# The two norms of a transformer block taken apart: raw x is transposed, g scales the transposed operand, rstd scales the products

## The chip, the cores and the metric

The kernel runs on one core of a Trainium2 chip. Its time is device time in microseconds (us). TensorE (PE) multiplies, VectorE (DVE) and ScalarE (ACT) do elementwise work, GpSimd (POOL) takes a small share of it, and SyncE (SP) issues the DMA transfers.

## What is computed

Two transformer blocks run one after the other over 256 tokens of width 1024, each with two layers, all in float32. The change touches the second block, whose layer is:

```python
def _rmsnorm(x, g):
    return x * lax.rsqrt(jnp.mean(x * x, axis=-1, keepdims=True) + NORM_EPS) * g

def _layer(x, ...):
    h = _rmsnorm(x, g_mix)
    proj = h @ w_in          # queries, keys, values of three attentions, gates
    ...
    x = x + y @ w_out
    h2 = _rmsnorm(x, g_mlp)
    x = x + jnp.square(jax.nn.relu(h2 @ w_up)) @ w_down
    return x
```

After the second layer a last rmsnorm with g_final gives the output. In what follows rstd is the factor rsqrt(mean(x²)+eps), one number for each token, and g is one number for each of the 1024 channels.

## The kernel before

**Tiles.** The 256 tokens are two tiles of 128 (tb 0 and 1), and each 1024 wide row is two halves of 512 (c 0 and 1). A float32 product is three matmuls on operands split into a high and a low part (mm3, L290 to L292). A split is an ACT copy that rounds to the high part (L297) and a DVE subtraction that leaves the low part (L298). Since TensorE contracts over partitions, the normed x has to be transposed before it is an operand: transposed4 (L441) puts four 128x128 transposes into a PSUM bank ("sm" in the rows), and the split reads that bank.

**Weights.** They stream in units of 512 KB (128 x 1024), loaded six units ahead of use and split three ahead: ACT copies (L265), DVE subtracts (L267). A table SLOW gives the subtraction of four units at each place between two stages to POOL instead of DVE. The ACT copy of such a unit is what releases the POOL subtraction.

**The norm.** norm_g(x, hT, tb, g) does everything for one token tile: sum_sq squares both halves on ACT (L430), rms_scale adds the two sums (L435) and runs six more operations on 128x1 tiles for rsqrt on DVE (L409, L413, L418, L413, L420, L421); then for each half DVE writes x * rstd * g (L570), PE transposes it (L441), and ACT and DVE split it (L297, L298). It is called at four places, which I call B1 to B4:

- B1, from the first block into the second (ev_out, L1216 to L1226). Here the residual add (L1224) itself needs an rms_scale of the first block's own norm first.
- B2, from attention to MLP in layer 0 (ev_out, residual add L1725).
- B3, from the MLP of layer 0 to the attention of layer 1 (end, residual add L1776).
- B4, from attention to MLP in layer 1 (as B2).

**Order.** In proj(), token tile 1 runs a few weight units behind tile 0 (lag), so that tile 0's first matmuls of the next stage can cover tile 1's norm. A scheduler decides the order of the instructions of each engine when the program is built, from the written order and its own estimates; on the chip each engine runs its queue strictly in that order.

Of the kernel before, what the change touches and what calls it, by code (L numbers as in the profile page):

```python
# [100 lines left out]
def two_block_kernel(ctx: ExitStack, tc: tile.TileContext, A, out):  # L101
# [299 lines left out]

    def rsqrt(v, n, c):
# [18 lines left out]
        dve.scalar_tensor_tensor(y, t, 5.0 * r ** 4, y, op0=ALU.add, op1=ALU.mult)  # L421
        return y

# [7 lines left out]

    def rms_scale(sq, n=1):
# [3 lines left out]
        return rsqrt(v, n, D ** 0.5)  # L436

# [125 lines left out]

    def norm_g(x, hT, tb, g):
        sq = small(2)
        sum_sq(x, sq)
        rs = rms_scale(sq, 1)
        for c in range(2):
            xn = t2([P, 512])
            dve.scalar_tensor_tensor(xn, x[c], rs, g[c], op0=ALU.mult, op1=ALU.mult)  # L570
            yield from transpose_half(hT, tb, c, xn)

# [249 lines left out]
    def block1_layer(l, hT, xin, t_norm):  # L822
# [387 lines left out]
        def ev_out(c, tb, ps):  # L1210
# [9 lines left out]
            if last:  # L1220
                x = new[tb]
                rs = rms_scale(sqs[i][:, 0:2], 1)
                for c in range(2):
                    dve.scalar_tensor_tensor(x[c], osb.pop((tb, c)), rs, x[c], op0=ALU.mult, op1=ALU.add)  # L1224
                run(norm_g(x, nxt, tb, g_mix0))
            elif i == 1:  # L1226
                tbs = (2 * s, 2 * s + 1)
                g = update_affine([new[t] for t in tbs], [[osb.pop((t, c)) for c in range(2)] for t in tbs],
                                  sqs[s], nxt, s, mods)
                if s == 0:  # L1230
                    run(g)
                else:
                    later.append(spawn(g))

        if last:
            g_mix0 = load_g(A["g_mix_2"][0])
        proj(4, ya, ev_out, groups=2, lag={1: LAGB} if last else {2: LAG0, 3: LAG0})
        return nxt, new, later

# [63 lines left out]

    def merge_tok(bi, acts, waits, oT, operands, y, yT):


        for c in range(2):
            gt = {}

            def ev_gate(tb, ps):  # L1310
                t = gt[tb] = t2([P, 512])
                act.activation(t, ps, AF.Tanh, scale=0.5)
            if c == 0:
# [83 lines left out]

    def block2_layer(l, hT):
        acts = {tb: hT.stat(tb) for tb in range(2)}

        brT = {}
# [47 lines left out]
        def qc_task(tb, z):  # L1449
# [6 lines left out]
            for i in range(2):  # L1456
                split(*(t[:, :, tb * P:(tb + 1) * P] for t in qcT[i]), pt[:, 2 * i:2 * i + 2])

        def ev_qc(tb, ps):
            z = t2([P, 512])  # L1460
            act.activation(z, ps, AF.Copy, scale=0.125)
            t_c.append(spawn(qc_task(tb, z)))
# [9 lines left out]
        tailT = t2([P, 256])  # L1472
        act.activation(tailT, ps, AF.Copy)
        tail = {}
# [107 lines left out]
        def ev_qb(q, ps):  # L1582
            split(*qbT[q], ps, scale=0.125)
        projT(4, hT.mov, ev_qb)

        def ev_kb(q, ps):
            for j in range(2):
                r = slice(64 * j, 64 * j + 64)
# [29 lines left out]

        def ev_qa(q, ps):
            for j in range(2):  # L1620
                r = slice(64 * j, 64 * j + 64)
                split(*(t[r, :, j] for t in qbdA[q]), ps[r], scale=0.125)
        projT(4, hT.mov, ev_qa)
        kaT = [(t2([P, 2, 256], F32R), t2([P, 2, 256], F32R)) for _ in range(2)]

        def ev_ka(q, ps):
            split(*kaT[q], ps)
        projT(4, hT.mov, ev_ka)
        va = {}
# [124 lines left out]
        def down(f, uT, lag):  # L1754
            w = {}
            for step in range(4 + lag):
# [4 lines left out]
                for tb in range(2):  # L1761
# [7 lines left out]
                    for k in range(2):  # L1769
# [107 lines left out]
```

## Time and profile before

| | |
|---|---|
| Time, median of 3 runs | 1871.62 us (1869.54 to 1873.0) |
| Profiled execution | 1872.96 us, of which span 1871.1 us |
| Mean granted TensorE clock | 0.990 of full speed |
| Busy time of PE / DVE / ACT / POOL | 1817.4 / 1217.6 / 872.9 / 200.9 us |
| Share of the 16 DMA engines | 44.5% |

The span runs from the first to the last recorded instruction. Busy time is summed over an engine's instructions. PE is busy in 97% of the span, so what can be gained is what PE waits for, plus what it loses at a lower clock. All rows below are from the one profiled execution.

### The profile page before, as it was taken

The numbers are of one execution on the slowest core, as the hardware profiler recorded it, in microseconds if no ns is written. First come the engines' busy times: TensorE is split into PE (matmuls) and PEld (weight loads), VectorE is DVE, ScalarE is ACT, GpSimd is POOL, SyncE is SP. The second block draws the span as 40 slices with busy tenths as digits, with TensorE's granted clock in tenths as the row PEclk, the third lists the DMA queues.
The fourth block names the chain that finished last, engine by engine and source line by source line (L and its number), as shares of the span: only waits on it lengthen the run. The fifth ranks groups of instructions, "written<-read, shape, count | busy, mean of one in ns | idle before, by whom it ended". The sixth has DMA issues, their size and how long they took to land.

```text
span 1871.1 us, 25763 instructions
## 1 busy us (share of the span) xinstructions
PE 1817.4 (97%) x9696; PEld 1520.0 (81%) x9696; DVE 1217.6 (65%) x2356; ACT 872.9 (47%) x1507; POOL 200.9 (11%) x135
## 2 busy tenths in 40 slices
PE   8999999999999999999989999999998999989998
PEld 4888888887887878878878887789987878779997
DVE  4754546567876744578779886555567988655555
ACT  4623233445334433465455675434455567534443
POOL 2020000001101110001020033100012003220000
PEclk9999999999999999999999999999999999999999
DMA  9433224323463332446733355545553345554552
GB/s 354 142 124 120 94 70 131 104 91 113 147 214 102 120 102 78 146 139 213 257 124 136 126 180 170 178 147 187 185 187 134 122 141 171 180 168 147 191 182 100
DMA packets 80604, 281.42 MB, mean 150 GB/s; under 512 B 9824, under 2 KB 10208, under 8 KB 80352
## 3 DMA queue, kind: packets, MB, share of 16 engines
q1 hardware_dynamic: 80480, 279.78, 44.5%
q8 instruction: 76, 1.25, 0.3%
q14 instruction: 48, 0.39, 0.1%
HBM read 278.69 MB, written 1.05 MB: 150 GB/s over the span
## 4 chain that ended last, share of the span: by engine, by line
PE 74%; DVE 9%; ACT 2%; issue 1%; POOL 1%; DVEq 0%; ACTq 0%; POOLq 0%
PE mm L290 19%; PE mm L291 18%; PE mm L292 18%; PE sm L290 3%; PE sm L291 3%; PE sm L292 3%; DVE k L267 2%; PE sm L441 1%; PE sm L1155 1%; PE sm L1128 1%; POOL k L1684 1%; PE sm L1393 1%; DVE nw_t L413 1%; PE sm L1382 1%; DVE k L1556 1%
## 5 line engine op out<-in xcount | busy, mean ns | idle before, releaser
L290 PE MATMUL mm<-k,k 128*128 128x512 f32 (+1 forms) x2192 | 837.2, 382 | 2.2 <-ACT k L465 2.2
L291 PE MATMUL mm<-k,k 128*128 128x512 f32 (+1 forms) x2192 | 824.6, 376 | 0.9 <-POOL k L267 0.9
L292 PE MATMUL mm<-k,k 128*128 128x512 f32 (+1 forms) x2192 | 824.1, 376 | 1.1 <-DVE k L267 0.8
L267 DVE TENSOR_TENSOR k<-k,k 128x1024 fp32r<-128x1024 f32 x437 | 541.5, 1257 | 184.4 <-ACT k L265 120.0
L265 ACT ACTIVATE k<-k 128x1024 fp32r<-128x1024 f32 x458 | 474.3, 1056 | 346.0 <-DVE k L267 138.1
L290 PEld LDWEIGHTS mm<-k,k 128*128 128x128 f32 x2192 | 415.3, 190 | 77.5 <-issue 5.8
L292 PEld LDWEIGHTS mm<-k,k 128*128 128x128 f32 x2192 | 414.6, 189 | 76.5 <-DVE k L467 1.3
L291 PEld LDWEIGHTS mm<-k,k 128*128 128x128 f32 x2192 | 415.5, 190 | 70.2 <-POOL k L267 1.8
L290 PE MATMUL sm<-k,k 128*128 128x256 f32 (+1 forms) x504 | 148.5, 295 | 0.0
L291 PE MATMUL sm<-k,k 128*128 128x256 f32 (+1 forms) x504 | 146.5, 291 | 0.0
L292 PE MATMUL sm<-k,k 128*128 128x256 f32 (+1 forms) x504 | 145.8, 289 | 0.0
L267 POOL TENSOR_TENSOR k<-k,k 128x1024 fp32r<-128x1024 f32 x21 | 51.5, 2472 | 463.4 <-ACT k L265 351.2
L290 PEld LDWEIGHTS sm<-k,k 128*128 128x128 f32 x504 | 96.7, 192 | 3.6 <-issue 2.4
L1749 DVE TENSOR_TENSOR k<-k 128x512 f32<-128x512 f32 x28 | 19.3, 688 | 121.7 <-ACT k L1748 121.7
L291 PEld LDWEIGHTS sm<-k,k 128*128 128x128 f32 x504 | 96.6, 192 | 2.0 <-issue 0.3
L292 PEld LDWEIGHTS sm<-k,k 128*128 128x128 f32 x504 | 96.6, 192 | 1.0
L619 DVE CUSTOM_DVE_ANT_0 k<-k,k 128x1024 f32<-128x1024 f32 x56 | 68.9, 1234 | 22.6 <-PE mm L291 20.2
L1748 ACT ACTIVATE k<-sm 128x512 f32<-128x512 f32 x28 | 16.5, 590 | 131.5 <-PE sm L292 131.5
L297 ACT ACTIVATE k<-sm 128x256 fp32r<-128x256 f32 (+2 forms) x102 | 41.2, 410 | 77.1 <-PE sm L441 50.9
L298 DVE TENSOR_TENSOR k<-sm,k 128x256 fp32r<-128x256 f32 (+2 forms) x102 | 45.7, 458 | 37.1 <-ACT k L297 30.3
L441 PE MATMUL sm<-cst,k 128*128 128x128 f32 x232 | 38.3, 293 | 23.5 <-DVE k L570 20.0
L441 PEld LDWEIGHTS sm<-cst,k 128*128 128x128 f32 x232 | 29.1, 150 | 35.2 <-issue 25.9
(284 smaller groups left out, 1577.9 us busy)
## 6 DMA issues: line engine op xcount, KB each, us to landing
k<-in_w_in SPq DMA_DIRECT2D x248, 512.0 KB, 3.5
k<-in_w_up SPq DMA_DIRECT2D x64, 512.0 KB, 4.4
k<-in_w_down SPq DMA_DIRECT2D x64, 512.0 KB, 3.5
k<-in_w_bo SPq DMA_DIRECT2D x48, 512.0 KB, 3.5
k<-in_w_modT SPq DMA_DIRECT2D x32, 512.0 KB, 3.5
k<-in_w_out SPq DMA_DIRECT2D x32, 512.0 KB, 3.6
k<-in_w_mod SPq DMA_DIRECT2D x16, 512.0 KB, 9.6
k<-in_c_rows SPq DMA_DIRECT2D x5, 512.0 KB, 3.7
```

The costliest lines, as they stand in the source:

```text
L265: act.activation(h, r, AF.Copy)
L267: (pool if i in slow else eng).tensor_tensor(lo, r, h.bitcast(F32), op=ALU.subtract)
L290: pe.matmul(ps, lh, rh, start=start, stop=False)
L291: pe.matmul(ps, lh, rl, start=False, stop=False)
L292: pe.matmul(ps, ll, rh, start=False, stop=stop)
L297: act.activation(h, src, AF.Copy)
L298: dve.tensor_tensor(lo, src, h.bitcast(F32), op=ALU.subtract)
L413: dve.scalar_tensor_tensor(t, y, y, v, op0=ALU.mult, op1=ALU.mult)
L441: pe.transpose(ps[:, k], src[:, k * P:(k + 1) * P], ident)
L619: dve.tensor_tensor_reduce(o, w, sb[s], 0.5, 0.0, op0=ALU.mult, op1=ALU.add, accum_out=res[:, s, i - 1:i])
L1128: pe.matmul(ps[m], a[r, h], b[r], start=(i == 0), stop=(i == 2))
L1749: dve.tensor_tensor(r, r, r, op=ALU.mult)
```

## The change

The norm is no longer applied to x before the transposes.

- scaled_half transposes the raw half of x right after its residual add. g then scales the transposed form, where a channel lies on a partition, as a scale operand of the split. As g differs for each group of 128 channels, the one ACT copy and the one DVE subtraction of 128x512 become four of each of 128x128, in pairs.
- rstd of a token is applied later, to the products. Where a product has tokens on partitions, the ACT copy out of PSUM takes rstd as its scale. Where it has tokens along the free axis (qb, kb, qa, ka, tail, and seven of eight up-projections), rstd has to lie along the free axis too: spread() transposes the broadcast rstd with two PE transposes and an ACT copy, and a DVE operation multiplies the PSUM by that row. For qb, kb, qa and ka this is an added operation (scaled()); in the up-projections the pair relu on ACT and square on DVE becomes relu with scale on DVE and square on ACT.
- The g vectors of block 2 are loaded as one tile g2 in channel-on-partition form by four small DMAs (in place of eight 256 KB broadcasts).

```diff
+    class Rms:
+        def set(self, x, tb):
+            sq = small(2)
+            sum_sq(x, sq)
+            rms_scale(sq, 1, self(tb))
+            dve.tensor_scalar(self(tb, True), self(tb), 0.5, None, op0=ALU.mult)
+        def spread(self, lead):
+            def task():
+                yield from wait(lead)
+                ps = sm_bank()[:, :256]
+                for tb in range(2):
+                    pe.transpose(ps[:, tb * P:(tb + 1) * P], self(tb).to_broadcast([P, P]), ident)
+                yield
+                self.b = t2([P, 256])
+                act.activation(self.b, ps, AF.Copy)
+            self.task = spawn(task())
...
+    def scaled_half(hT, tb, c, x, g):
+        ps = transposed4(x)
+        hh, hl = hT.dst(tb, c)
+        for k in range(4):
+            gk = g[:, 4 * c + k:4 * c + k + 1]
+            act.activation(hh[:, k], ps[:, k], AF.Copy, scale=gk)
+            dve.scalar_tensor_tensor(hl[:, k], ps[:, k], gk, hh[:, k].bitcast(F32), op0=ALU.mult, op1=ALU.subtract)
...
                     dve.scalar_tensor_tensor(x[c], osb.pop((tb, c)), rs, x[c], op0=ALU.mult, op1=ALU.add)
-                run(norm_g(x, nxt, tb, g_mix0))
+                    scaled_half(nxt, tb, c, x[c], g2[:, 0])
+                rms.set(x, tb)
...
+    g2 = cp.tile([P, 2 * DEPTH, KT], F32, name="g2")
+    for l in range(DEPTH):
+        for i, w in enumerate(("g_mix_2", "g_mlp_2")):
+            sp.dma_start(g2[:, 2 * l + i], A[w][l].rearrange("(k p) -> p k", p=P))
...
+        def scaled(ps, scale=1.0):
+            o = t2([P, 2, 256])
+            dve.scalar_tensor_tensor(o, ps, scale, rms.row()[:, None, :].to_broadcast([P, 2, 256]),
+                                     op0=ALU.mult, op1=ALU.mult)
+            return o
...
-            split(*qbT[q], ps, scale=0.125)
+            split(*qbT[q], scaled(ps, 0.125))
...
-            act.activation(vb[tb], ps, AF.Copy)
+            act.activation(vb[tb], ps, AF.Copy, scale=rms(tb))
...
+        def residual(tb, c, ps, hT, g, r):
             xs = xb[tb][c]
             dve.tensor_tensor(xs, ps, xs, op=ALU.add)
+            scaled_half(hT, tb, c, xs, g)
             if c == 1:
-                run(norm_g(xb[tb], h2, tb, g))
+                r.set(xb[tb], tb)
...
                     r = t2([P, 2, 256])
-                    act.activation(r, ps, AF.Relu)
-                    dve.tensor_tensor(r, r, r, op=ALU.mult)
+                    dve.scalar_tensor_tensor(r, ps, 0.0, rms_h.row()[:, None, :].to_broadcast([P, 2, 256]),
+                                             op0=ALU.max, op1=ALU.mult)
+                    act.activation(r, r, AF.Square)
```

**What moves in the instruction order.** The lines of the changed kernel differ: L603 and L604 are the ACT and the DVE half of a pair in scaled_half, L431 is sum_sq, L436, L409, L413, L418, L420 and L422 are rms_scale with its rsqrt, L579 is 0.5 * rstd, L442 is transposed4, L1775 is the residual add at B2 to B4. In the names, k_933 to k_936 are x (tile 0 c 0, tile 0 c 1, tile 1 c 0, tile 1 c 1).

ACT at B3, before: first all of tile 0's norm and split, then the copies (L265) of three of the four POOL units, among tile 1's squares.

```order
L430 ACTIVATE k_2472_12435,small_12434<-k_933_4669 128x512
L430 ACTIVATE k_2473_12437,small_12434<-k_934_4670 128x512
L297 ACTIVATE k_2479_12456<-sm_12451 128x4x128
L297 ACTIVATE k_2483_12467<-sm_12462 128x4x128
L265 ACTIVATE k_2486_12473<-k_2462_12396 128x1024
L430 ACTIVATE k_2495_12516,small_12515<-k_935_4673 128x512
L430 ACTIVATE k_2496_12518,small_12515<-k_936_4674 128x512
L265 ACTIVATE k_2489_12485<-k_2465_12408 128x1024
```

ACT at the same place in the changed kernel; the four L265 here are those of the four POOL units.

```order
L431 ACTIVATE k_2479_12523,small_12522<-k_933_4669 128x512
L603 ACTIVATE k_2470_12484<-sm_12479,g_5095 128x128
L265 ACTIVATE k_2473_12496<-k_2460_12442 128x1024
L603 ACTIVATE k_2470_12484<-sm_12479,g_5095 128x128
L431 ACTIVATE k_2480_12525,small_12522<-k_934_4670 128x512
L603 ACTIVATE k_2470_12484<-sm_12479,g_5095 128x128
L603 ACTIVATE k_2476_12512<-sm_12507,g_5095 128x128
L265 ACTIVATE k_2485_12540<-k_2463_12454 128x1024
L603 ACTIVATE k_2470_12484<-sm_12479,g_5095 128x128
L603 ACTIVATE k_2476_12512<-sm_12507,g_5095 128x128
L265 ACTIVATE k_2488_12552<-k_2466_12466 128x1024
```

The copies of POOL units now stand among tile 0's pairs, ahead of tile 1's squares; the first of the four, which before stood ahead of all of this, stands here too.

DVE at B3, before: tile 0's rsqrt chain, its two L570, its two splits, and the adds of tile 1 between them.

```order
L418 SCALAR_TENSOR_TENSOR nw_y_12441<-nw_t_12442,nw_y_12441 128x1
L413 SCALAR_TENSOR_TENSOR nw_t_12442<-nw_y_12441,small_12439 128x1
L420 SCALAR_TENSOR_TENSOR nw_t_12442<-nw_t_12442 128x1
L421 SCALAR_TENSOR_TENSOR nw_y_12441<-nw_t_12442,nw_y_12441 128x1
L570 SCALAR_TENSOR_TENSOR k_2477_12449<-k_933_4669,nw_y_12441,k_2230_10854 128x512
L570 SCALAR_TENSOR_TENSOR k_2481_12460<-k_934_4670,nw_y_12441,k_2231_10855 128x512
L298 TENSOR_TENSOR k_2480_12457<-sm_12451,k_2479_12456 128x4x128
L1776 TENSOR_TENSOR k_935_4673<-mm_11085,k_935_4673 128x512
L298 TENSOR_TENSOR k_2484_12468<-sm_12462,k_2483_12467 128x4x128
L1776 TENSOR_TENSOR k_936_4674<-mm_11105,k_936_4674 128x512
```

DVE at the same place in the changed kernel.

```order
L436 SCALAR_TENSOR_TENSOR small_12527<-small_12522 128x1
L409 TENSOR_SCALAR nw_y_12529<-small_12527 128x1
L604 SCALAR_TENSOR_TENSOR k_2471_12485<-sm_12479,g_5095,k_2470_12484 128x128
L604 SCALAR_TENSOR_TENSOR k_2477_12513<-sm_12507,g_5095,k_2476_12512 128x128
L413 SCALAR_TENSOR_TENSOR nw_t_12530<-nw_y_12529,small_12527 128x1
L418 SCALAR_TENSOR_TENSOR nw_y_12529<-nw_t_12530,nw_y_12529 128x1
L413 SCALAR_TENSOR_TENSOR nw_t_12530<-nw_y_12529,small_12527 128x1
L420 SCALAR_TENSOR_TENSOR nw_t_12530<-nw_t_12530 128x1
L422 SCALAR_TENSOR_TENSOR rms_10910<-nw_t_12530,nw_y_12529 128x1
L579 TENSOR_SCALAR rms_10910<-rms_10910 128x1
L604 SCALAR_TENSOR_TENSOR k_2471_12485<-sm_12479,g_5095,k_2470_12484 128x128
L604 SCALAR_TENSOR_TENSOR k_2477_12513<-sm_12507,g_5095,k_2476_12512 128x128
```

Right behind the last of these rows stands the add of tile 1, c 0 (L1775, k_935). No operation of the rsqrt chain leads to an operand of the matmuls any more, but the whole chain of tile 0 still stands ahead of tile 1's adds in DVE's queue, now among the pairs. At B2 and B4 the order is alike, with the c 0 add of tile 1 between the first L413 and L418.

PE at B3, before: tile 1's transposes (the bank's name is the one that tile 1's splits read) stand behind 18 matmuls of the next stage.

```order
L292 MATMUL mm_12556<-k_2486_12473,k_2484_12468 128x512
L290 MATMUL mm_12556<-k_2486_12473,k_2483_12467 128x512
L291 MATMUL mm_12556<-k_2487_12474,k_2483_12467 128x512
L292 MATMUL mm_12556<-k_2486_12473,k_2484_12468 128x512
L441 MATMUL sm_12532<-cst,k_2500_12530 128x128 x4
L290 MATMUL mm_12556<-k_2489_12485,k_2483_12467 128x512
L441 MATMUL sm_12541<-cst,k_2502_12539 128x128 x4
```

PE at the same place in the changed kernel.

```order
L290 MATMUL mm_11163<-k_2464_12456,k_2430_12236 128x512
L442 MATMUL sm_12575<-cst,k_935_4673 128x128 x4
L291 MATMUL mm_11163<-k_2465_12457,k_2430_12236 128x512
L292 MATMUL mm_11163<-k_2464_12456,k_2431_12237 128x512
L290 MATMUL mm_12632<-k_2467_12468,k_2470_12484 128x512
L291 MATMUL mm_12632<-k_2468_12469,k_2470_12484 128x512
L292 MATMUL mm_12632<-k_2467_12468,k_2471_12485 128x512
L290 MATMUL mm_12632<-k_2467_12468,k_2470_12484 128x512
L291 MATMUL mm_12632<-k_2468_12469,k_2470_12484 128x512
L442 MATMUL sm_12595<-cst,k_936_4674 128x128 x4
```

Tile 1's transposes moved ahead: c 0's two matmuls before the end of the down-projection (mm_11163), c 1's five matmuls into the next stage (mm_12632). Less work of PE lies ahead of them.

## Rows read from the trace of the kernel before

**Rows 1.** Waits of PE, 918 to 1871 us: total, times, longest.

```profile
PE sm L441 <- DVE k L570: 20.0, 6, 6.1
PE sm L1382 <- DVE k L1377: 2.3, 2, 1.2
```

**Rows 2.** Windows: us; busy (instructions) of PE, PEld, DVE, ACT, POOL; PEclk; DMA.

```profile
918.00:956.00 38.00, 30.51 (x133) 24.08 (x131) 27.11 (x54) 15.91 (x29) 12.13 (x7) 0.91 0.27 85
956.00:1196.00 240.00, 236.69 (x1313) 196.20 (x1312) 189.61 (x425) 141.80 (x255) 41.51 (x31) 1.00 0.48 159
1196.00:1225.00 29.00, 24.79 (x110) 20.07 (x109) 16.02 (x27) 9.94 (x17) 7.06 (x3) 0.94 0.37 127
...
1388.00:1416.00 28.00, 22.86 (x96) 18.43 (x95) 16.76 (x32) 9.64 (x18) 12.41 (x7) 0.88 0.30 97
...
1660.00:1690.00 30.00, 25.78 (x112) 20.91 (x111) 16.60 (x28) 10.27 (x19) 7.06 (x3) 0.89 0.39 123
```

**Rows 3.** Timeline at B3, DVE: start, us, instruction, idle before.

```profile
1392.74 0.69 DVE L1776 TENSOR_TENSOR k<-mm,k 128x512 f32<-128x512 f32 x1 [4.33 <-PE mm L292]
...
1399.91 0.68 DVE L1776 TENSOR_TENSOR k<-mm,k 128x512 f32<-128x512 f32 x1
...
1403.61 2.35 DVE L413 SCALAR_TENSOR_TENSOR nw_t<-nw_y,small 128x1 f32<-128x1 f32 x1
1406.00 2.26 DVE L418 SCALAR_TENSOR_TENSOR nw_y<-nw_t,nw_y 128x1 f32<-128x1 f32 x1
...
1408.94 1.41 DVE L570 SCALAR_TENSOR_TENSOR k<-k,nw_y,k 128x512 f32<-128x512 f32 x2
```

**Rows 4.** Timeline at B3, POOL.

```profile
1400.96 2.41 POOL L267 TENSOR_TENSOR k<-k,k 128x1024 fp32r<-128x1024 f32 x1 [10.30 <-ACT k L265]
```

**Rows 5.** Timeline at B3, PE.

```profile
1409.84 1.09 PE L441 MATMUL sm<-cst,k 128*128 128x128 f32 x4 [4.88 <-DVE k L570]
```

**Rows 6.** Timeline at B2, all engines.

```profile
1212.01 7.06 POOL L267 TENSOR_TENSOR k<-k,k 128x1024 fp32r<-128x1024 f32 x3 [20.93 <-ACT k L265]
...
1212.70 0.69 DVE L1725 TENSOR_TENSOR k<-mm,k 128x512 f32<-128x512 f32 x1 [0.96 <-PE mm L292]
...
1214.66 2.13 DVE L413 SCALAR_TENSOR_TENSOR nw_t<-nw_y,small 128x1 f32<-128x1 f32 x1
...
1220.67 0.63 PE L441 MATMUL sm<-cst,k 128*128 128x128 f32 x4 [4.15 <-DVE k L570]
```

**Rows 7.** Timeline at B1, DVE.

```profile
938.89 2.12 DVE L413 SCALAR_TENSOR_TENSOR nw_t<-nw_y,small 128x1 f32<-128x1 f32 x1
...
944.01 1.42 DVE L1224 SCALAR_TENSOR_TENSOR k<-k,nw_y,k 128x512 f32<-128x512 f32 x2
...
947.70 1.42 DVE L570 SCALAR_TENSOR_TENSOR k<-k,nw_y,k 128x512 f32<-128x512 f32 x2
```

**Rows 8.** Timeline at B1, PE.

```profile
948.59 1.94 PE L441 MATMUL sm<-cst,k 128*128 128x128 f32 x8 [6.12 <-DVE k L570]
950.37 0.80 PE L290 MATMUL mm<-k,k 128*128 128x512 f32 x1
```

**Rows 9.** Groups by form, DVE: count, busy us, mean ns, idle before.

```profile
L1170 DVE SCALAR_TENSOR_TENSOR k<-k,nw_y,k 128x128 f32<-128x128 f32 x24 | 7.9, 389 | 0.0
```

**Rows 10.** Groups by form, ACT.

```profile
L265 ACT ACTIVATE k<-k 128x1024 fp32r<-128x1024 f32 x458 | 474.3, 1056 | 346.0 <-DVE k L267 138.1 <-PE mm L291 83.1 <-DVE mres L619 42.7
...
L1013 ACT ACTIVATE k<-cst,lg 128x128 f32<-128x128 f32 x32 | 9.8, 390 | 0.0
```

**Rows 11.** The transposes L441, 918 to 1871 us: min/median/max ns.

```profile
L441 PE MATMUL sm<-cst,k x112: 270/273/447, 933.3 to 1696.9; 128*128 128x128 f32 x112
```

**Rows 12.** Windows of the start, columns as in Rows 2.

```profile
11.00:12.00 1.00, 0.98 (x4) 0.14 (x4) 0.06 (x1) 0.00 (x0) 0.00 (x0) 1.00 0.99 388
12.00:13.00 1.00, 0.79 (x6) 0.14 (x4) 0.00 (x0) 0.00 (x0) 0.00 (x0) 1.00 1.07 237
...
50.00:60.00 10.00, 10.00 (x49) 8.32 (x48) 6.58 (x19) 6.54 (x10) 0.00 (x0) 1.00 0.05 18
```

More of the change, by code (lines that the diff above doesn't have):

```diff
@@ L400, in projT, with rsqrt @@
                     tick()
-    def rsqrt(v, n, c):
+    def rsqrt(v, n, c, out=None):
         m, k = RSQRT[c]
@@ L420, in rsqrt @@
         dve.scalar_tensor_tensor(t, t, 10.0 / 3.0 * r ** 2, t, op0=ALU.subtract, op1=ALU.mult)
-        dve.scalar_tensor_tensor(y, t, 5.0 * r ** 4, y, op0=ALU.add, op1=ALU.mult)
-        return y
+        o = y if out is None else out
+        dve.scalar_tensor_tensor(o, t, 5.0 * r ** 4, y, op0=ALU.add, op1=ALU.mult)
+        return o
     def small(n, tag="small"):
@@ L430, in sum_sq, with rms_scale @@
             act.activation(t2([P, 512]), x[c], AF.Square, accum_out=sq[:, c * n + i:c * n + i + 1])
-    def rms_scale(sq, n=1):
+    def rms_scale(sq, n=1, out=None):
         v = small(n)
         dve.scalar_tensor_tensor(v, sq[:, 0:n], D * EPS, sq[:, n:2 * n], op0=ALU.add, op1=ALU.add)
-        return rsqrt(v, n, D ** 0.5)
+        return rsqrt(v, n, D ** 0.5, out)
     def transposed4(src):
@@ L562, in update_affine, with __init__, __call__, row @@
                 yield
[L564 to L571, printed above, removed]
+    class Rms:
+        def __init__(self):
+            self.r = T(tp, [P, 2, 2], "rms", bufs=2)
+        def __call__(self, tb, half=False):
+            return self.r[:, tb, int(half):int(half) + 1]
+        def set(self, x, tb):
[13 more added lines that the diff above has]
+            self.task = spawn(task())
+        def row(self):
+            join([self.task])
+            return self.b
+    def scaled_half(hT, tb, c, x, g):
[5 more added lines that the diff above has]
+            dve.scalar_tensor_tensor(hl[:, k], ps[:, k], gk, hh[:, k].bitcast(F32), op0=ALU.mult, op1=ALU.subtract)
     sel = C("sel")
@@ L1235, in block1_layer @@
         if last:
-            g_mix0 = load_g(A["g_mix_2"][0])
+            rms = Rms()
         proj(4, ya, ev_out, groups=2, lag={1: LAGB} if last else {2: LAG0, 3: LAG0})
-        return nxt, new, later
+        return nxt, new, rms if last else later
     class Ys:
@@ L1302, in merge, with merge_tok @@
             projT(2, operands, ev_o, n=n, ticks=1)
-    def merge_tok(bi, acts, waits, oT, operands, y, yT):
+    def merge_tok(bi, acts, waits, oT, operands, y, yT, rms=None):
         for c in range(2):
@@ L1456, in qc_task @@
             for i in range(2):
-                split(*(t[:, :, tb * P:(tb + 1) * P] for t in qcT[i]), pt[:, 2 * i:2 * i + 2])
+                split(*(t[:, :, tb * P:(tb + 1) * P] for t in qcT[i]), pt[:, 2 * i:2 * i + 2], scale=0.125)
         def ev_qc(tb, ps):
             z = t2([P, 512])
-            act.activation(z, ps, AF.Copy, scale=0.125)
+            act.activation(z, ps, AF.Copy, scale=rms(tb))
             t_c.append(spawn(qc_task(tb, z)))
@@ L1472, in block2_layer @@
         tailT = t2([P, 256])
-        act.activation(tailT, ps, AF.Copy)
+        dve.tensor_tensor(tailT, ps, rms.row(), op=ALU.mult)
         tail = {}
@@ L1582, in ev_qb @@
         def ev_qb(q, ps):
-            split(*qbT[q], ps, scale=0.125)
+            split(*qbT[q], scaled(ps, 0.125))
         projT(4, hT.mov, ev_qb)
         def ev_kb(q, ps):
+            ps = scaled(ps)
             for j in range(2):
@@ L1619, in ev_qa @@
         def ev_qa(q, ps):
+            ps = scaled(ps, 0.125)
             for j in range(2):
                 r = slice(64 * j, 64 * j + 64)
-                split(*(t[r, :, j] for t in qbdA[q]), ps[r], scale=0.125)
+                split(*(t[r, :, j] for t in qbdA[q]), ps[r])
         projT(4, hT.mov, ev_qa)
@@ L1626, in ev_ka @@
         def ev_ka(q, ps):
-            split(*kaT[q], ps)
+            split(*kaT[q], scaled(ps))
         projT(4, hT.mov, ev_ka)
@@ L1717, in block2_layer, with ev_out @@
         for bi, b in enumerate(MERGE2):
-            merge_tok(bi, acts, waits[b], [], lambda tb, b=b: by_block(brT[b])(tb), y, yT)
+            merge_tok(bi, acts, waits[b], [], lambda tb, b=b: by_block(brT[b])(tb), y, yT, rms)
         ya = {tb: yT.stat(tb) for tb in range(2)}
-        g = load_g(A["g_mlp_2"][l])
-        h2 = Acts(True)
-        def ev_out(c, tb, ps):
+        h2, rms_h = Acts(True), Rms()
+        def residual(tb, c, ps, hT, g, r):
             xs = xb[tb][c]
             dve.tensor_tensor(xs, ps, xs, op=ALU.add)
+            scaled_half(hT, tb, c, xs, g)
             if c == 1:
-                run(norm_g(xb[tb], h2, tb, g))
+                r.set(xb[tb], tb)
+        def ev_out(c, tb, ps):
+            residual(tb, c, ps, h2, g2[:, 2 * l + 1], rms_h)
         proj(4, ya, ev_out, groups=2, lag={1: LAG1})
         acc = {}
+        rms_h.spread(4)
         def up(f):
@@ L1774, in down @@
                     if f == 7 and k2 == 1:
+                        if not last:
+                            residual(tb, c, acc[tb, c], nxt, g2[:, 2 * l + 2], rms_n)
+                            continue
                         xs = xb[tb][c]
@@ L1778, in down @@
                             end(tb)
-        nxt = Acts(True)
+        nxt, rms_n = Acts(True), Rms()
         last = l == DEPTH - 1
-        g_end = load_g(A["g_final_2"] if last else A["g_mix_2"][l + 1])
+        if last:
+            g_end = load_g(A["g_final_2"])
         def end(tb):
-            if not last:
-                run(norm_g(xb[tb], nxt, tb, g_end))
-                return
             sq = small(2)
@@ L1800, in block2_layer @@
             down(f, us.pop(f), LAGD if f == 7 else 0)
-        return nxt
+        return nxt, rms_n
     for l in range(DEPTH):
-        h_acts = block2_layer(l, h_acts)
+        h_acts, rms2 = block2_layer(l, h_acts, rms2)
 def layout(inputs):
```

14 lines of the change are left out of this document (8 added, 6 removed).

## The prediction

> **What bounds the kernel now.** PE is busy 97% of the span, so I look first at what stops it where the change applies, from 918 us to the end. In the waits of PE one pair stands out: the transposes of normed x wait for the last step of the norm, L570, 20.0 us in six waits; the next largest is 2.3 [rows 1]. The windows say where. The four places B1 to B4 are the stretches in which PE's busy time falls short of the window: 7.5 us (38 - 30.51), 4.2, 5.1 and 4.2, together 21 [rows 2]. In those windows the granted clock is also lower, 0.91, 0.94, 0.88 and 0.89, against 1.00 in the 240 us between B1 and B2, where PE hardly stops. The missing clock times the window's length is at most 3.4, 1.7, 3.4 and 3.3 us, 11.8 in all; part of it lies inside the stop, so it is an upper bound. About 21 us of stops and some of 12 us of clock is all that removing the norm could give.
>
> Then the timelines, to see what PE waits for. At B3 tile 1's c 0 add starts at 1399.91, but its norm's first L570 only at 1408.94, and PE stops for 4.88 us [rows 3, 5]. Nearly half of those 9 us are two operations on 128x1 tiles: L413 takes 2.35 us and L418 2.26. They run while POOL does its share of the weight splits; a POOL piece takes 2.41 us [rows 4], and at B2 three of them back to back 7.06 [rows 6]. L413 there takes 2.13, yet the add L1725, which reads PSUM and SBUF, starts inside the same 7.06 us and takes its 0.69. So the stop is half norm arithmetic and half small operations that read two SBUF tiles and are held up by POOL.
>
> **The change part by part.**
>
> *Removed: norm before the transposes.* Tile 1's operands no longer wait for squares, rsqrt and L570. That is what could give the 21 us. It does so only if the add itself comes as early as before, and it stands in DVE's queue behind what was put there.
>
> *Moved: tile 0's rsqrt chain against POOL.* Before, ACT first split all of tile 0, and three of the four weight copies that release POOL came after it; tile 0's chain ran beside an idle POOL. In the changed order these copies stand among tile 0's pairs, and DVE has tile 0's L436, L413, L418 still ahead of tile 1's c 0 add. At B3: c 0's add starts at 1392.74 [rows 3]; add 0.69, transposes some 0.6 (two medians of 0.273 [rows 11]), one copy of 0.39, one L265 of 1.06 [rows 10], and POOL starts at about 1395.5 to 1395.8. Four pieces of about 2.4 follow, released one by one by the other copies. L436 lands on the first, L413 on the second, L418 on the third, so DVE is free at 1395.8 + 3 x 2.4 = about 1403. Then come four small operations (some 0.8) and two half-pairs of 0.39 [rows 9]: tile 1's add at about 1404.6 against 1399.91 before. PE, which reaches tile 1's c 0 transposes shortly before 1399.9 (two matmuls before the end of the down-projection that this add waits for), stops until 1404.6 + 0.69, or 5.4 us; some of it may lie beside the two matmuls left. Before it was 4.88, and the gap of the window was 5.1. I take -0.5 for B3 (minus is a loss). The bounds: +5.1 of stop and some clock, say +6.4, if no small operation meets POOL; -2 if a fourth one does.
>
> *B2 and B4.* The same happens more mildly, since tile 1's c 0 add now stands ahead of L418 and only its c 1 add behind it. One or two of the 2.1 to 2.4 us stalls fall ahead of that. Walking the order with these durations I get four PE stops of 0.35, 0.35, 0.2 and 2.1, or 3.0 against 4.15 [rows 6]. That is 1.15 each, and I add about a quarter of the clock loss of the two windows (0.4 and 0.8), as the shorter stops may spare some of it: +1.55 and +1.95. Bounds for each: -1.6 (a second stall ahead of the c 1 add) and +4.
>
> *B1.* The residual add there needs the first block's own norm, and that chain stays: L413 still 2.12, L1224 at 944.01 [rows 7]. What falls away is the second chain from there to L570 at 947.70. Tile 1's c 0 half is ready at 944.01 + 0.71 = 944.72 (half of L1224's two). Transposes (two medians, 0.55) and the first pair (0.78) bring the first matmul of tile 1 to about 946.1, in place of 950.37 [rows 8]: +4.2, with bounds 0.5 (if the pairs then hold PE back) and 5.5.
>
> *Added: pairs of 128x128.* A half's split is now four ACT copies of 0.39 and four DVE operations of 0.39, which take turns: 0.78 for a pair, 3.1 us a half [rows 9, 10]. Before it was one of each of 128x512, some 1.4 at L1725's 0.69 [rows 6]. Cover: PE has six matmuls for each group of 128 channels and token tile, and needs one group at a time, so it mostly keeps up. I take nothing beside the walk above; if the cover goes, 1.7 us for a half.
>
> *Added: spread.* Four calls of two transposes, eight in all, at 0.273 each and 0.1 at the least (my estimate, if four overlap as at 948.59: eight in 1.94 us at the lower clock) [rows 8, 11]: 0.8 to 2.2 us of PE, I take 1.4. Their wait for rstd is hidden behind eight or four units of matmuls.
>
> *Added: scaled().* 16 operations from PSUM to SBUF, at L1725's 0.69 [rows 6]: 11 us of DVE, 5.5 a layer, in a stage where DVE is busy 189.61 of 240 us and PE stops for 3.3 in all [rows 2]. DVE goes from 79 to 81%. I take -0.7, bounds 0 and -3. In the up-projections a DVE and an ACT operation swap places: as many operations as before on engines that are busy 65% and 47% of the span, so nothing. Scales on ACT copies that are there anyway cost nothing on the path: ACT is the less busy engine.
>
> *Loads.* g2's four transfers are 4096 elements of 4 bytes, 128 x 8 each, and the order puts their issue among the loads of the start. The row for such packets is the window from 12 to 13 us: 640 short packets pass (g_pre, b_mod, positions, b_forget), and the rate falls from 388 to 237 GB/s at a full share [rows 12], or 0.4 us of stream. 4096 packets then cost 2.5 us. Cover: at 50 to 60 us the share is 0.05, so the stream has run ahead by then. Nothing for the sum; without cover 2.5, and if one transfer is slow on its own, more. The eight broadcasts of 256 KB that fall away are hidden already.
>
> **The sum.** 4.2 + 1.55 + 1.95 - 0.5 - 1.4 - 0.7 = 5.1 us. The profiled execution took 1872.96 (span 1871.1 and 1.86 around it) and would take 1867.9. The median of the runs lies 1.34 lower; from 1871.62 I get **1866.5**.
>
> **A rule weighed.** The row: 128x1 operations with two SBUF inputs take 2.13 to 2.35 us under POOL's subtraction, the add with one input from PSUM 0.69 [rows 3, 6]. The Trainium skill, "SBUF — State Buffer", section "Who interferes with whom", states it as a lock: a DVE instruction with two SBUF inputs contends with a GpSimd instruction that reads SBUF, and whoever issues first holds the port for the whole instruction. It speaks against this change, as the chain meets the lock wherever it stands: by it B3 stays at about -0.5. If the stall were one of tile 1's place alone, B3 would give +6.4, and the time would be about 1860. The trace agrees with the rule as far as it shows; tile 0's place under POOL no run has shown yet.
>
> **The rivals.**
> (a) *The wait just goes.* No small operation of tile 0 meets POOL, because POOL's copies come late enough in fact. Then B1 +5, B2 and B4 +4 each, B3 +6.4, less 2.1: about 17 us, 1854 to 1855. For it: the operands depend on the chain no more. Against it: POOL's releases stand ahead of tile 1's adds in the order. Chance 0.15.
> (b) *The stall moves whole.* Two or three stalls of 2.4 us stand ahead of tile 1's adds at each of B2, B3 and B4, and the stop comes back: B1 +3, B2 and B4 about -0.5 each, B3 -1.5, less 2.1: -1.6, or 1870 to 1875, same within what can be told. For it: the order at B3. Against: the milder one at B2. Chance 0.29.
> (c) *Slower: pairs.* Each ACT half of a pair waits for the DVE half before it, behind weight splits in both queues. From the point where a half's 3.1 us end later than PE's work ahead of it, each place pays 1.7 us for tile 0's and 1.7 for tile 1's last half, 13.6 in all, less the 7.2 that the four places give, plus the 2.1 of spread and scaled: 8.5 slower, or 1880, with 1876 to 1882 around it. For it: four places with sixteen halves and no slack shown for them. Against: PE needs one group of channels at a time. Chance 0.11.
> (d) *The start.* g2's transfers hold the weight units behind them, and PE with them. At 2.5 us this turns the forecast into 1869; it ends slower than before only if the packets cost over three times what the 12 to 13 us window shows, 8.8 us or more, 1875 and up. Chance 0.03.
> The forecast itself, 1861 to 1870, has 0.42.
>
> **How the numbers follow.** 0.2%, or 3.7 us, is about what a measurement of this kernel can tell from no change. Faster by more (under 1867.9): (a) whole and most of the forecast's range, 0.15 + 0.34 = 0.49. Same (1867.9 to 1875.4): the rest of the forecast and nearly all of (b), 0.36. Slower: (c), (d) and an end of (b), 0.15. The range takes in most of (a) and reaches into (c): 1854 to 1878. The likeliest case's own range is 1861 to 1870.
>
> **What the profile will show.** Right: no L570 and no wait of PE on it; PE's transposes of tile 1 wait for the residual adds, about 3 us at B1, 2 to 3 at B2 and B4, about 5 at B3; there a 128x1 operation of tile 0 of over 2 us ahead of the add L1775; POOL's pieces starting while tile 0's pairs run. Eight short transposes of L587; and 16 operations of scaled() (L1445) of about 0.69 each on DVE. Wrong if tile 0's small operations take 0.2 us throughout (then a), if PE waits on L604 or L603 rather than L1775 (then c), or if the span up to 918 us has changed by more than 1 us (then d).

## The result and the profile after

The changed kernel took 1860.88 us (median of 4 runs, 1858.64 to 1863.72), the kernel before 1870.95; the ratio is 0.9946, with a 95% interval of 0.9929 to 0.9963. It is faster by about 10.1 us, where 5.1 were forecast. The profiled execution took 1861.23 us, with a span of 1859.4.

The waits of PE from 918 us on, after (total, times, longest), as in [rows 1]:

```profile
PE sm L442 <- DVE k L1775: 6.9, 3, 4.5
PE sm L442 <- DVE k L1257: 3.1, 1, 3.1
PE sm L442 <- DVE k L1794: 2.6, 2, 1.4
PE sm L1739 <- POOL k L1734: 2.5, 4, 1.0
```

The 20.0 us on L570 have become 6.9 on the residual adds of B2 to B4, 3.1 on the add of B1 (L1257) and 2.6 on L1794, the square in the first up-projection, which did not show before. The wait on L1734, POOL's part of a split in the attention, is 2.5 in place of 0.5. The windows at B1, the attention of layer 0, B2, B3 and B4 (columns as in [rows 2]):

```profile
915.00:953.00 38.00, 34.78 (x157) 28.34 (x156) 28.14 (x69) 20.66 (x45) 12.37 (x8) 0.96 0.36 117
953.00:1190.00 237.00, 233.26 (x1294) 192.56 (x1293) 186.55 (x427) 136.87 (x246) 38.46 (x30) 1.00 0.47 152
1190.00:1221.00 31.00, 28.55 (x136) 23.04 (x135) 22.95 (x45) 20.23 (x39) 9.51 (x4) 1.00 0.48 153
1384.00:1410.00 26.00, 21.49 (x94) 17.15 (x93) 20.65 (x45) 16.61 (x35) 12.13 (x7) 0.87 0.34 107
1651.00:1684.00 33.00, 30.45 (x144) 24.54 (x143) 23.06 (x46) 21.30 (x40) 9.52 (x4) 1.00 0.51 167
```

The granted clock at B2 and B4 is 1.00, against 0.94 and 0.89 before, and PE misses 2.5 us of each window instead of 4.2. At B1 it is 0.96 against 0.91, with 3.2 us missing instead of 7.5; at B3 0.87 against 0.88, with 4.5 us missing. So B1, B2 and B4 changed and B3 did not.

At B3, the timeline of DVE after (start, us, instruction):

```profile
1387.34 1.59 DVE L436 SCALAR_TENSOR_TENSOR small<-small 128x1 f32<-128x1 f32 x1 [0.26 <-ACT k L431]
...
1389.56 1.75 DVE L413 SCALAR_TENSOR_TENSOR nw_t<-nw_y,small 128x1 f32<-128x1 f32 x1
1391.34 2.26 DVE L418 SCALAR_TENSOR_TENSOR nw_y<-nw_t,nw_y 128x1 f32<-128x1 f32 x1
...
1394.86 0.68 DVE L1775 TENSOR_TENSOR k<-mm,k 128x512 f32<-128x512 f32 x1
```

POOL at the same place, after:

```profile
1386.52 7.07 POOL L267 TENSOR_TENSOR k<-k,k 128x1024 fp32r<-128x1024 f32 x3 [175.49 <-DVE k L1775]
```

PE there, after:

```profile
1395.60 1.12 PE L442 MATMUL sm<-cst,k 128*128 128x128 f32 x4 [4.51 <-DVE k L1775]
```

This is the forecast's picture. Three of POOL's pieces now run beside tile 0's chain, its L436, L413 and L418 take 1.59, 1.75 and 2.26 us, and the add of tile 1 (1394.86) stands behind them. POOL starts 2.9 us after tile 0's c 0 add (1383.62), forecast 2.8 to 3.1; tile 1's add starts 11.2 us after it, forecast 11.9. PE stops for 4.51 us, forecast "about 5 at B3".

At B2, the timeline of DVE after:

```profile
1201.29 0.68 DVE L1775 TENSOR_TENSOR k<-mm,k 128x512 f32<-128x512 f32 x1
...
1202.08 2.27 DVE L413 SCALAR_TENSOR_TENSOR nw_t<-nw_y,small 128x1 f32<-128x1 f32 x1
...
1208.24 0.68 DVE L1775 TENSOR_TENSOR k<-mm,k 128x512 f32<-128x512 f32 x1
```

PE there, after:

```profile
1208.97 0.66 PE L442 MATMUL sm<-cst,k 128*128 128x128 f32 x4 [1.20 <-DVE k L1775]
...
1218.83 0.66 PE L442 MATMUL sm<-cst,k 128*128 128x128 f32 x4 [1.25 <-DVE k L1794]
```

Tile 1's c 0 add came before any stall. One operation, the second L413, took 2.27, and PE stopped for only 1.20 us on tile 1's c 1 add (1208.24).

**Where the 10 us are.** To place them I cut each trace at the same instructions: the last read behind L619 of the first block, the copy L1512 in each attention (L1560 in the changed kernel, where L619 is L652), and the first residual add at B2, B3, B4 and at the end. The times between them, in us (the column "again" is a second trace of the kernel before, from the first experiment):

| stretch | before | again | after | forecast of gain | gain against the mean of both |
|---|---|---|---|---|---|
| start to L619 | 901.1 | 898.1 | 898.5 | 0 | 1.1 |
| B1 and first projections, to L1512 | 94.7 | 95.6 | 90.4 | 4.2 | 4.75 |
| rest of attention, layer 0 | 199.3 | 199.4 | 200.0 | part of -2.1 | -0.65 |
| B2 and MLP, layer 0 | 197.5 | 198.4 | 194.7 | 1.55 | 3.25 |
| B3 and first projections, to L1512 | 66.6 | 66.2 | 66.8 | -0.5 | -0.4 |
| rest of attention, layer 1 | 199.4 | 199.4 | 200.0 | part of -2.1 | -0.6 |
| B4 and MLP, layer 1 | 198.2 | 198.4 | 194.8 | 1.95 | 3.5 |
| end | 14.2 | 14.2 | 14.2 | 0 | 0 |

Without the start, the gains add up to 9.85 us. The start of the changed kernel differs from the first trace by 2.6 us, more than the 1 us that was named as a sign of (d), but it is shorter and not longer, and experiment 1 shows as much between two traces of one kernel.

### The profile page after: what moved, and what is told of

Its sections match the earlier page's. It is cut to its first block, busy times and chain, and to the rows that moved or that the text cites. A ratio compares the mean times of both kernels' runs of the same rounds, so it can differ in the third digit from the quotient of the medians.

```text
span 1859.4 us, 25881 instructions
## 1 busy us (share of the span) xinstructions
PE 1813.5 (98%) x9704; PEld 1516.0 (82%) x9704; DVE 1218.9 (66%) x2414; ACT 888.1 (48%) x1557; POOL 200.0 (11%) x135
## 3 DMA queue, kind: packets, MB, share of 16 engines
q8 instruction: 76, 1.25, 0.3%
## 4 chain that ended last, share of the span: by engine, by line
PE 40%; DVE 8%; ACT 2%; POOL 2%; issue 1%; DMA 0%; DVEq 0%; POOLq 0%; ACTq 0%
PE mm L290 9%; PE mm L291 9%; PE mm L292 9%; PE sm L290 3%; PE sm L292 3%; PE sm L291 3%; DVE k L267 2%; POOL k L1734 1%; PE sm L442 1%; PE sm L1432 1%; PE sm L1421 1%; ACT k L265 1%; POOL k L1732 1%; DVE k L1604 1%; DVE nw_t L413 1%
## 5 line engine op out<-in xcount | busy, mean ns | idle before, releaser
L267 DVE TENSOR_TENSOR k<-k,k 128x1024 fp32r<-128x1024 f32 x437 | 547.4, 1269 | 185.0 <-ACT k L265 123.0
L265 ACT ACTIVATE k<-k 128x1024 fp32r<-128x1024 f32 x458 | 475.1, 1056 | 329.2 <-DVE k L267 142.9
L1803 DVE SCALAR_TENSOR_TENSOR k<-sm,k 128x512 f32<-128x512 f32 x28 | 19.4, 692 | 123.4 <-PE sm L292 123.4
L1805 ACT ACTIVATE k<-k 128x512 f32<-128x512 f32 x28 | 17.4, 622 | 140.0 <-DVE k L1803 140.0
L652 DVE CUSTOM_DVE_ANT_0 k<-k,k 128x1024 f32<-128x1024 f32 x56 | 68.8, 1233 | 23.4 <-PE mm L291 20.3
L913 POOL TENSOR_TENSOR k<-k,k 128x512 f32<-128x512 f32 x16 | 23.4, 1467 | 289.9 <-DVE k L911 289.0
L298 DVE TENSOR_TENSOR k<-sm,k 128x256 fp32r<-128x256 f32 (+2 forms) x78 | 31.8, 413 | 31.4 <-ACT k L297 30.6
L442 PE MATMUL sm<-cst,k 128*128 128x128 f32 x232 | 37.5, 287 | 15.2 <-DVE k L1775 6.9
L442 PEld LDWEIGHTS sm<-cst,k 128*128 128x128 f32 x232 | 28.3, 146 | 27.6 <-DVE k L1775 10.1
```

What stands on the lines that cost most here:

```text
L265: act.activation(h, r, AF.Copy)
L267: (pool if i in slow else eng).tensor_tensor(lo, r, h.bitcast(F32), op=ALU.subtract)
L298: dve.tensor_tensor(lo, src, h.bitcast(F32), op=ALU.subtract)
L442: pe.transpose(ps[:, k], src[:, k * P:(k + 1) * P], ident)
L652: dve.tensor_tensor_reduce(o, w, sb[s], 0.5, 0.0, op0=ALU.mult, op1=ALU.add, accum_out=res[:, s, i - 1:i])
L913: pool.tensor_tensor(o, o, tt, op=ALU.add)
```

## The experiments

**1. The kernel before once more**, to see what two traces of one kernel differ by.

> The kernel before, unchanged, for a second trace of it. The trace of the changed kernel reaches the end of the first block 2.6 us earlier than the first trace of before, by two stretches in which the clock falls at another moment. If that is chance, this trace lies somewhere between and its time at 900 us differs from the first by up to 2 us either way; if the changed instruction order gives it, this trace repeats the first within 0.5 us there. Ratio 1.000 within 0.2%.

Measured: ratio 0.9998 (0.9989 to 1.0008), span 1869.7. It reaches the mark of L619 at 898.1, 3.0 us ahead of the first trace. 1.7 of them are there by the first read behind L619, at 105 us, and stay the same up to 529 us; the windows from 20 to 30 us show where they arise (columns as in [rows 2]). In the first trace of before:

```profile
20.00:25.00 5.00, 3.30 (x12) 2.10 (x12) 2.69 (x11) 3.93 (x10) 2.07 (x3) 1.00 1.02 417
25.00:30.00 5.00, 4.15 (x20) 1.05 (x20) 2.92 (x4) 1.65 (x3) 3.66 (x2) 0.67 1.04 418
```

In the second trace:

```profile
20.00:25.00 5.00, 3.95 (x10) 2.81 (x11) 2.55 (x12) 4.03 (x10) 2.07 (x3) 0.72 1.02 414
25.00:30.00 5.00, 4.73 (x33) 2.53 (x32) 3.08 (x4) 2.25 (x4) 3.81 (x2) 0.94 1.02 411
```

In one the granted clock fell between 25 and 30 us (0.67), in the other for the most part between 20 and 25 (0.72). The other 1.3 us arise behind 529 us, where the clock falls in both, to 0.54 from 610 to 615 us in the first and to 0.59 from 605 to 610 in the second. So a difference of 2.6 us at the start is chance, as the first of the two theories had it. The clock at the four places is chance in part too. In the second trace of before, at B2 and at B3:

```profile
1194.00:1223.00 29.00, 24.77 (x108) 20.11 (x107) 15.61 (x27) 9.84 (x17) 7.05 (x3) 0.89 0.40 127
1386.70:1414.70 28.00, 22.75 (x104) 18.27 (x102) 17.44 (x33) 10.31 (x18) 12.42 (x7) 0.94 0.29 95
```

It is 0.89 and 0.94 here, 0.94 and 0.88 in the first trace, at nearly the same busy time of PE.

**2 and 3. All weight splits on DVE**, in the kernel before and in the changed one.

```diff
-    SLOW = [(1, 2, 3, 4), (1, 2, 3, 4), (1, 2, 3, 4), (1, 2, 3, 4)]
+    SLOW = [(), (), (), ()]
```

> Before, with all weight splits on DVE (SLOW empty). Theory (POOL's splits hold small DVE operations with two SBUF inputs): no L413, L418 or L435 over 0.5 us at B1 to B4, and tile 1's norm 4.5 us shorter; but DVE has three more splits of 1.26 us there, so the stops of PE fall from 20.0 in sum to 8 to 14, and the time by 5 to 10 us. Rival (the small operations are late for another cause, such as the squares): some of them still take over 1 us, and the stops stay near 20.

> The changed kernel with all weight splits on DVE. Theory: the stop of 4.5 us at B3 falls to under 2.5, as no small operation of tile 0 is held up ahead of tile 1's add, and the stops at B2 and B4 (1.2) go or become splits on DVE; 0 to 5 us faster than the changed kernel, ratio to before 0.992 to 0.995. Rival (the norm's chain is not what holds the add, the pairs are): B3's stop stays at 4 or more.

Measured: 1848.46 us for before without POOL's share, ratio 0.9879 (0.9863 to 0.9896); 1839.48 us for the changed kernel without it, 0.9825 (0.9810 to 0.9839). Both are far beyond what I expected. The operation L413 (min/median/max ns) in before without POOL's share:

```profile
L413 DVE SCALAR_TENSOR_TENSOR nw_t<-nw_y,small x24: 211/219/221, 917.9 to 1841.5; 128x1 f32<-128x1 f32 x24
```

In the changed kernel without it:

```profile
L413 DVE SCALAR_TENSOR_TENSOR nw_t<-nw_y,small x24: 208/216/222, 919.7 to 1832.9; 128x1 f32<-128x1 f32 x24
```

In the changed kernel as it is:

```profile
L413 DVE SCALAR_TENSOR_TENSOR nw_t<-nw_y,small x24: 208/219/2393, 924.9 to 1854.3; 128x1 f32<-128x1 f32 x24
```

Without POOL's share none takes longer than 222 ns, where it was up to 2393. The waits of PE in before without POOL's share:

```profile
PE sm L441 <- DVE k L570: 11.0, 6, 7.1
```

The waits of PE in the changed kernel without it:

```profile
PE sm L1739 <- POOL k L1734: 2.6, 4, 1.0
PE sm L1421 <- DVE k L1416: 2.2, 2, 1.1
PE sm L442 <- DVE k L1257: 0.9, 1, 0.9
```

In before, 11.0 us on L570 stay, 7.1 of it at B1; in the changed kernel 0.9, on the add of B1. The stalls of the small operations came from POOL's share of the splits. Some of the gain, 8 and 5 us, lies ahead of B1, where the mark of L619 is reached at 891.4 and 893.3: the same table gives POOL three splits at the second layer of the first block, at 593 us, and PE's stop of 4.92 at 611.44, behind it, is gone in both. Without POOL's share the change gains 9.0 us: 8.0 at B1 (the stretch to L1512 goes from 95.1 to 87.1) and 1.7, 1.4 and 1.9 at B2, B3 and B4, less 1.3 and 1.1 in the two attention stretches and 1.9 at the start. So at B3, too, the change gains where no operation is held up.

**4. One rsqrt chain for both tiles**, after tile 1's last add.

```diff
-        def set(self, x, tb):
-            sq = small(2)
-            sum_sq(x, sq)
-            rms_scale(sq, 1, self(tb))
-            dve.tensor_scalar(self(tb, True), self(tb), 0.5, None, op0=ALU.mult)
+        def set(self, x):
+            sq = small(4)
+            for tb in range(2):
+                sum_sq(x[tb], sq, tb, 2)
+            rms_scale(sq, 2, self.r[:, :, 0])
+            dve.tensor_scalar(self.r[:, :, 1], self.r[:, :, 0], 0.5, None, op0=ALU.mult)
...
-                rms.set(x, tb)
+                if tb == 1:
+                    rms.set(new)
...
-            if c == 1:
-                r.set(xb[tb], tb)
+            if c == 1 and tb == 1:
+                r.set(xb)
```

> The changed kernel, with one rsqrt chain for both tiles (128x2) after tile 1's last add, so that at B2 to B4 no small operation stands ahead of tile 1's adds; POOL's share stays. Theory: B3's stop goes from 4.5 to under 1, B2's and B4's from 1.2 to under 0.5, and 5 to 8 us fall away: 1853 to 1856, ratio to before 0.990 to 0.992. Rival (the adds wait for pairs and POOL's copies anyway): B3's stop stays over 3 and the time within 2 us of the changed kernel's.

Measured: 1855.34 us, ratio 0.9908 (0.9894 to 0.9923), 5.5 us under the changed kernel. No stop on the adds is left at B2 to B4, and their stretches are shorter by 2.0, 1.5 and 2.0 us. At B3 a smaller loss replaced the stop. DVE there in this kernel:

```profile
1390.94 2.26 DVE L436 SCALAR_TENSOR_TENSOR small<-small 128x2 f32<-128x2 f32 x1 [0.26 <-ACT k L431]
1393.23 2.65 DVE L409 TENSOR_SCALAR nw_y<-small 128x2 int32<-128x2 int32 x1
```

PE there in this kernel:

```profile
1402.10 0.33 PE L1480 MATMUL sm<-cst,k 128*128 128x128 f32 x1 [3.76 <-DVE k L1476]
```

The chain now starts late and is itself held up twice, so tile 0's projection waits for rstd and PE stops for 3.76 us behind it.

**5. One split for a half** in place of the four pairs, without g.

```diff
-        for k in range(4):
-            gk = g[:, 4 * c + k:4 * c + k + 1]
-            act.activation(hh[:, k], ps[:, k], AF.Copy, scale=gk)
-            dve.scalar_tensor_tensor(hl[:, k], ps[:, k], gk, hh[:, k].bitcast(F32), op0=ALU.mult, op1=ALU.subtract)
+        split(hh, hl, ps)
```

> The changed kernel with one ACT copy and one DVE subtraction of 128x512 for a half in place of four pairs of 128x128; g of the two norms is left out. Theory (PE needs one group of channels at a time, the pairs cost little by themselves, POOL's hold does): B2 and B4 gain at most 1 us each, B3's stop stays at 4 or more. Rival (the pairs' taking turns delays the adds and the operands): the stretches from B2 to B3 and from B4 to the end get 2 to 4 us shorter each.

Measured: 1865.42 us in one run, so not faster, and B3's stop stayed at 4.3; the 2 to 4 us a stretch that the rival promises did not come. The run does not isolate the pairs, as the order changed with them: at B2 and B4 three small operations (L418, L420, L422, 2.27 to 2.35 us each) now stood ahead of tile 1's c 1 add in place of one, and the stop grew from 1.20 to 3.2. PE at B2 in this kernel:

```profile
1211.04 1.12 PE L442 MATMUL sm<-cst,k 128*128 128x128 f32 x4 [3.17 <-DVE k L1772]
...
1212.38 0.63 PE L292 MATMUL mm<-k,k 128*128 128x512 f32 x1
1212.81 0.63 PE L290 MATMUL mm<-k,k 128*128 128x512 f32 x1
```

PE at B4 in this kernel:

```profile
1675.94 0.66 PE L442 MATMUL sm<-cst,k 128*128 128x128 f32 x4 [3.20 <-DVE k L1772]
...
1676.66 0.40 PE L292 MATMUL mm<-k,k 128*128 128x512 f32 x1
1676.90 0.39 PE L290 MATMUL mm<-k,k 128*128 128x512 f32 x1
```

The two stops are alike, but after the first the matmuls run 0.43 us apart, after the second 0.24. The windows behind the two stops:

```profile
1211.00:1216.00 5.00, 4.96 (x14) 4.10 (x15) 4.86 (x11) 3.24 (x6) 0.00 (x0) 0.50 0.17 40
1676.00:1681.00 5.00, 5.00 (x25) 4.20 (x26) 4.79 (x12) 3.12 (x5) 0.00 (x0) 1.00 0.25 102
```

The granted clock is half in the one and full in the other. From B2 to B3 this kernel took 198.2 us, from B4 to the end's first add 195.4, against 194.7 and 194.8 in the changed kernel. So behind two stops of one size the stretches differ by 2.7 us, and the clock that follows differs with them.

**6. scaled() twice**, one of the two results unused.

```diff
             dve.scalar_tensor_tensor(o, ps, scale, rms.row()...
+            o2 = t2([P, 2, 256])
+            dve.scalar_tensor_tensor(o2, ps, scale, rms.row()...
-            return o
+            return o2
```

> The changed kernel with each of the 16 operations of scaled() done twice, the second into an unused tile. Theory (the 0.6 us that each layer's attention lost is scaled() on DVE): each attention stretch after the mark gets 0.5 to 1.5 us longer again, most of it at PE's wait for POOL's L1734, which reads what comes behind qa and ka. Rival (the loss is spread's transposes and moved work): less than 0.2 us.

The edit hands on the second result, so what reads it waits for both operations. Measured: 1877.72 us in one run, 17 slower than the changed kernel. The rest of attention took 205.4 and 205.7 instead of 200.0, far more than the 0.5 to 1.5 that I expected, and the stretches to L1512, in which two of the eight scaled() of each layer fall, are longer by 2.8 and 2.1. The 16 added operations cost more than the 11 us that they keep DVE busy. PE's waits in layer 0's attention (from 956 to 1190 us) with the operation doubled:

```profile
PE sm L1421 <- DVE k L1416: 3.1, 2, 1.9
PE sm L1742 <- POOL k L1737: 1.3, 2, 1.0
PE mm L290 <- ACT k L1647: 1.2, 1, 1.2
PE sm L1432 <- DVE k L1425: 1.1, 1, 1.1
```

The same in the changed kernel (953 to 1185 us):

```profile
PE sm L1739 <- POOL k L1734: 1.2, 2, 1.0
PE sm L1421 <- DVE k L1416: 1.1, 1, 1.1
```

New stops stand at other places than the one I named, and the clock falls behind them. With the operation doubled, from 1050 to 1100 us:

```profile
1050.00:1100.00 50.00, 45.81 (x214) 33.12 (x212) 35.79 (x106) 31.54 (x77) 0.00 (x0) 0.93 0.32 106
```

PE misses 4.2 us there at a granted clock of 0.93; in the changed kernel it misses nothing from 1047 to 1097 us, at 1.00. The wait on POOL's L1734 (L1737 here) stayed as it was, 1.3 to 1.2.

**7. g2 set by a memset**, without g.

```diff
-    for l in range(DEPTH):
-        for i, w in enumerate(("g_mix_2", "g_mlp_2")):
-            sp.dma_start(g2[:, 2 * l + i], A[w][l].rearrange("(k p) -> p k", p=P))
+    pool.memset(g2, 1.0)
```

> The changed kernel with g2 set to 1 by a memset instead of the four element-wise transfers, so g of the two norms is left out. Theory (the transfers are hidden): the hole of 5 us at 86 GB/s in the DMA stream from 30 to 35 us goes, and PE reaches its last L617 at 45 to 48 us as before, the end of the first block within the 3 us that two traces of before differ by. Rival (the start pays for them): L617 comes 2 us or more earlier than 45.1.

Measured: 1860.61 us in one run. The window in which the transfers pass, in the changed kernel:

```profile
30.00:35.00 5.00, 4.21 (x21) 2.99 (x20) 2.44 (x7) 2.68 (x5) 0.00 (x0) 1.00 0.77 86
```

The same window here:

```profile
30.00:35.00 5.00, 4.23 (x22) 3.00 (x21) 2.69 (x7) 3.05 (x5) 0.00 (x0) 1.00 1.03 417
```

The loss is 5 us at 86 instead of 417 GB/s, or 4.0 us of stream (the prediction had 2.5), and it is nearly all hidden: PE reaches its last L617, a matmul of the start that reads loaded weights, at 44.77 instead of 45.13.

**8. Both: one chain, and no share of POOL.**

> The joint rsqrt chain together with all weight splits on DVE. Theory (the chain's place matters only through POOL's hold): nothing more to gain on the 1839.5 of the changed kernel without POOL, and up to 4 us to lose as tile 0's products wait for rstd: 1838 to 1844. Rival (a chain ahead of the adds costs by itself): 1834 to 1837.

Measured: 1838.90 us, ratio 0.9829 (0.9813 to 0.9846), the same as experiment 3. Without POOL's hold, the chain's place costs nothing that can be told.

## Why the prediction came out as it did

The direction, the range (1854 to 1878) and the places were right. The likeliest value was 5.6 us too high; the measured time lies just under its own range of 1861 to 1870. It lies beside the "about 1860" that the prediction gives for a stall of tile 1's place alone, but that is chance: B3, which would have given +6.4 there, gave -0.4, and the gain came at B2 and B4.

- **B1** was forecast at +4.2 and measured 4.75; PE's stop was 3.1, forecast about 3. Experiment 3 shows what limited it: with L413 at 0.2 us the stop is 0.9.
- **B3** was forecast at -0.5, measured -0.4, by the walk's mechanism. The rival (a), that the wait just goes, fell here. Experiments 3 and 4 took away the hold or the chain ahead of the adds, and the stop on the adds went each time.
- **B2 and B4** are the step that was mis-sized: "I add about a quarter of the clock loss of the two windows (0.4 and 0.8)". Measured were 3.25 and 3.5 in place of 1.55 and 1.95, nearer to the +4 of (a). The stops came to 2.45 and 2.55 against the forecast 3.0 (one stall, and a stop of 1.25 to 1.35 at L1794 that I had not seen), but the clock did not fall at all: 1.00 in both windows. This is no chance of one trace: experiments 6 and 7 have the changed order at B2 and B4 too, the clock there is 1.00 as well, and the stretch from B2 to B3 takes 194.7 us in all three. A full clock gives back at most 1.7 us at B2 (3.2 by the second trace of before, at 0.89) and 3.3 at B4 [rows 2], less what the spread costs. How much of the 3.25 and 3.5 is clock and how much is stop no run separates. Experiment 5 shows that behind a stop of 3.2 us the clock can go either way.
- **Costs.** scaled() and spread were put at -2.1; the two attention stretches lost 1.25, and 2.4 without POOL's share (experiments 2 and 3). "DVE goes from 79 to 81%" did not come, it is 78.7% (186.55 of 237 us), and it was the wrong measure of the price: experiment 6 shows that a second helping costs 17 us by stops and clock. No run takes scaled() out alone, so what the first helping costs is not shown.
- **Pairs and loads** cost nothing that can be seen. In the changed kernel PE waits on no L603 and no L604, the sign named for (c), and experiment 5 is not faster without the pairs; the loads are hidden (experiment 7). Rivals (c) and (d) fell.
- **The rule on the port.** The Trainium skill, "SBUF — State Buffer", section "Who interferes with whom", has the contention go by where the inputs lie (two of them in SBUF, against a GpSimd instruction that reads SBUF). The trace agrees, and it meets tile 0's operations as it met tile 1's: tile 0's L413 took 1.75 and 2.27 under POOL, and the adds from PSUM went through at 0.68.

What stays open: why the clock falls after one stop of 3.2 us and not after another, and what scaled() costs by itself.

## What to carry over

A chain taken off the path of the operands still delays them if it stands ahead of their producer in an engine's queue; look for the queue, not only for the data. Here it took both, the place in the queue and POOL's hold: with either one gone the stop on the adds went. Before taking work from a busy engine to GpSimd, count the small operations that run at the same time: the table that moved some 20 splits of 1.26 us cost 23 us in the kernel before, more than twice what this change gained, and the best kernels here are the changed one without it, in either order of the chain (1839.48 and 1838.90 us). A stop's price is the stop plus the clock that may follow, and which of the two comes is not settled by the stop's length.

## What the hardware showed unexpectedly

- Beside a memset of POOL, which reads nothing, a DVE operation was late too: in experiment 4, L409 on 128x2 took 2.65 us from 1393.23 on, while POOL ran its memsets L1463 and no split. POOL in that kernel:

```profile
1383.70 9.48 POOL L267 TENSOR_TENSOR k<-k,k 128x1024 fp32r<-128x1024 f32 x4 [175.45 <-DVE k L1777]
1393.12 2.73 POOL L1463 MEMSET k<- 128x1024 f32 x3
```

  The shape counts. L409 has one input, and beside POOL's splits it was late on 128x2, in the first block of the kernel before:

```profile
593.37 7.12 POOL L267 TENSOR_TENSOR k<-k,k 128x1024 fp32r<-128x1024 f32 x3 [46.28 <-PE mm L291]
595.84 2.33 DVE L409 TENSOR_SCALAR nw_y<-small 128x2 int32<-128x2 int32 x1
```

  On 128x1 it was not, at B3 in the changed kernel beside the splits that held L436 and L413:

```profile
1388.97 0.15 DVE L409 TENSOR_SCALAR nw_y<-small 128x1 int32<-128x1 int32 x1
```

  On 128x2 with POOL idle it took 0.17 us (605.71 in the kernel before). The Trainium skill, "SBUF — State Buffer", section "Who interferes with whom", says that tensor_scalar can enter the 2-port modes, when its operands meet their conditions, and then contends with GpSimd; this fits, but no run here shows the mode.
- A half-clock stretch does not follow from the length of the stop alone: 3.17 us was followed by 0.50, 3.20 by 1.00 (experiment 5).
